# Up projection and embedding gate in seven half-sized products, weight sums made in DRAM, up and down in groups

## The chip, the cores and the metric

The kernel runs on one core of a Trainium2 chip. The metric is the device time of one execution in microseconds, as the median of several runs. The engines are named as the profile names them: PE is TensorE (matmuls), PEld its weight loads, DVE VectorE, ACT ScalarE, POOL GpSimd, SP SyncE. "Software transfers" are the DMA transfers that POOL issues; SP issues the others.

## The reference

One layer of a decoder on x of 512 tokens by 1024 channels, all in float32. A mixer with three attention branches comes first, then an output projection, a LayerNorm (LN1), and the part that is changed here:

```python
for i in range(DEPTH):            # DEPTH = 1
    m = mixer(x, w_in[i], ...)                                   # ends with merged @ w_out
    x = layer_norm(DEEPNORM_ALPHA * x + m, ln1_g[i], ln1_b[i])
    hid = jax.nn.relu(x @ w_up[i])                               # 1024 -> 4096
    c = jnp.square(hid) @ w_down[i]                              # 4096 -> 1024
    ple = jax.nn.sigmoid(x @ w_ple_gate[i]) * (p[i] @ w_ple[i])  # gate 1024 -> 1024, p has 256 channels
    x = layer_norm(DEEPNORM_ALPHA * x + c + ple, ln2_g[i], ln2_b[i])
```

## The kernel before, in words

**Precision.** Every fp32 operand is split in two parts: a high part (a cast, ACT, L227 for weights) and a low part (the operand less its high part, DVE, L229). A product is three matmuls: high by high, high by low, low by high (`mm3`, L86 to L89). A matmul has 128 x 128 weights and up to 512 columns.

**Items.** The program is a list of items, one per product tile. An item has a function that emits its matmuls into one PSUM bank (`mm`) and one that empties the bank (`ev`), which the main loop emits one item later. PSUM has two banks with the tag `mm` and six with the tag `at`. Between items the loop advances the attention's generators (`step`) and, after the output projection, those of LN1 (`pending`).

**Weights.** `load` puts a 512 KB piece of weights in a list, `fill` (L169) issues the loads in that order on SP's queue into `RAW` = 4 buffers named `raw`, and `split_next` (L215) makes the high and low part (`wh`, `wl`, `RING` = 7 of each). `pump` calls both, at most seven pieces ahead of the items that are done with theirs.

**Order.** The mixer's items end at `wout_at`. Then come the per-layer embedding p @ w_ple (`ple_items`, 8 items of 6 matmuls), the output projection (`wout_items`, 8 of 24), the embedding's gate (`pleg_items`, 8 of 24), the MLP, and a plain block at its end (`plain`). After each 128 tokens of the output projection `ln1_gen` runs LN1, whose reciprocal root is a pow on POOL (L462), then transposes x1 and splits it into `x1hT` and `x1lT`.

**MLP.** The up projection has 32 items (`up`), each 128 hidden channels by 512 tokens in 24 matmuls of 512 columns; ACT does Relu and Square into `hid`. The down projection takes the hidden channels in seven blocks of 512 and a plain one. A block uses the seven-product scheme for a 2 x 2 block matrix (Strassen's, in Winograd's form): with A the hidden tile and B the weights, each cut in 2 x 2, seven products p = 1 to 7 of half size replace eight. Products of sums need sums of weights: `total` with `add` (L195 to L205) makes four of them per block on DVE, as `wsum` 128x1024 tiles. The sums of hidden tiles are made on DVE by `left_first` and `left_rest`. Up items stand between the down items one by one.

**Transfers on POOL.** One pT tile (`pTraw`, issued at `wout_at` - 9), and at `wout_at` - 1 the constants `ln_g`, `ln_b` and eight tiles `xn` of the residual. The pows of the differential attention (L1148) are on POOL as well.

Of the kernel before, what the change touches and what calls it, by code (L numbers as in the profile page):

```python
# [55 lines left out]
def trunk(tc, a, out):  # L56
    nc = tc.nc
    es = ExitStack()
    with es:
# [7 lines left out]
        NSLOT = 42  # L67
# [74 lines left out]
        RING, RAW, NSUM = 7, 4, 3  # L142
        ORDERED, AHEAD = 17, 4
        loads, sums, chunks, placed = [], [], [], []
        st = {"dma": 0, "sum": 0, "split": 0}
# [6 lines left out]
        def total(s1, s2):  # L152

            s = {"of": (s1, s2), "w": s1["w"], "uses": 0}
            s1["uses"] += 1
            s2["uses"] += 1
            sums.append(s)
            return s
# [10 lines left out]
        def fill():  # L169
            while st["dma"] < len(loads):  # L170
                s = loads[st["dma"]]
                if not s["own"]:
# [19 lines left out]
                add()  # L192
            add()

        def add():  # L195
            while st["sum"] < len(sums) and (st["sum"] < NSUM or sums[st["sum"] - NSUM]["uses"] == 0):
                s = sums[st["sum"]]
                if any("raw" not in x for x in s["of"]):
                    break
                r = ring.tile([P, 1024], F32, name=nm("wsum"), tag="wsum", bufs=NSUM)  # L200
                s["raw"] = r[:, :s["w"]]
                nc.vector.tensor_add(s["raw"], s["of"][0]["raw"], s["of"][1]["raw"])
                for x in s["of"]:
                    x["uses"] -= 1
                st["sum"] += 1  # L205
# [9 lines left out]
        def split_next():  # L215
# [9 lines left out]
            for h, lo, a0, a1 in parts:  # L225
                raw = c["from"]["raw"][:, a0:a1]
                i = nc.vector.tensor_copy(h, raw) if c.get("dve") else nc.scalar.copy(h, raw)  # L227
                st["cast"] = getattr(i, "ins", i)
                i = nc.vector.tensor_sub(lo, raw, h.bitcast(F32))  # L229
                st["low"] = getattr(i, "ins", i)  # L230
# [290 lines left out]

        def ln1_gen(tt):
# [4 lines left out]
            q = slice(tt * P, tt * P + P)  # L527
            if not x1T:
                bh = one.tile([P, 8, 512], F32R, name="x1hT", tag="XH", bufs=1)
                bl = one.tile([P, 8, 512], F32R, name="x1lT", tag="XL", bufs=1)  # L530
                for k in range(8):
                    x1T[k], x1Tl[k] = bh[:, k, :], bl[:, k, :]
                x1T["b"], x1Tl["b"] = bh, bl
            for h in range(2):
                tp = at_bank()
                for b in range(4):
                    nc.tensor.transpose(tp[:, b * P:b * P + P], x1[tt, h][:, b * P:b * P + P], ident)
                o = x1T["b"][:, 4 * h:4 * h + 4, q]
                t3 = tp.rearrange("p (k t) -> p k t", k=4)
                nc.scalar.copy(o, t3)  # L540
                nc.vector.tensor_sub(x1Tl["b"][:, 4 * h:4 * h + 4, q], t3, o.bitcast(F32))
            ln1_done[tt] = True
# [24 lines left out]
        def pleg_items():  # L567
            for half in range(2):
                cs = [chunk(a["wg"][half, c].rearrange("p k n -> p (k n)"), 1024) for c in range(4)]
                for tt in range(4):  # L570
                    def mm(ps, tt=tt, cs=cs):
                        for k in range(8):
                            c = cs[k // 2]
                            s = slice((k % 2) * 512, (k % 2) * 512 + 512)
                            q = slice(tt * P, tt * P + P)
                            nc.tensor.matmul(ps, x1T[k][:, q], c["h"][:, s], start=k == 0, stop=False)  # L576
                            nc.tensor.matmul(ps, x1T[k][:, q], c["l"][:, s], start=False, stop=False)  # L577
                            nc.tensor.matmul(ps, x1Tl[k][:, q], c["h"][:, s], start=False, stop=k == 7)

                    def ev(ps, tt=tt, half=half):  # L580
                        g = slot("sg2")
                        nc.scalar.activation(g, ps, AF.Sigmoid)
                        nc.vector.tensor_mul(g, g, ple.pop((tt, half)))
                        t = x1[tt, half]
                        nc.vector.scalar_tensor_tensor(t, t, ALPHA, g, op0=OP.mult, op1=OP.add)
                        acc[tt, half] = t
                        if half and tt > 1:
                            nc.vector.tensor_sub(acc[tt - 2, 1], acc[tt - 2, 1], t)
                    item(cs if tt == 3 else [], mm, ev, need=cs)

        hraw = {}
# [8 lines left out]
        def mlp_items():  # L605
            nb = 7

            def up(f, free=True):
                c = chunk(a["wu"][f].rearrange("p k m -> p (k m)"), 1024)

                def mm(ps):
                    for k in range(8):
                        s = slice(k * P, k * P + P)
                        mm3(ps, c["h"][:, s], c["l"][:, s], x1T[k], x1Tl[k], k == 0, k == 7)

                def ev(ps):
                    t = slot("hid")
                    nc.scalar.activation(t, ps, AF.Relu)
                    nc.scalar.activation(t, t, AF.Square)
                    left_rest()  # L620
                    if f >= 4 * nb:
                        left[f] = split(t)
                        return
                    hraw[f] = t
                    if f % 2:
                        left_first(f // 2)
                item([c] if free else [], mm, ev)
                return c

            def split(t, cols=slice(0, 512)):  # L630
                h = slot("hh", F32R)
                lo = slot("hl", F32R)
                nc.scalar.copy(h[:, cols], t[:, cols])
                nc.vector.tensor_sub(lo[:, cols], t[:, cols], h[:, cols].bitcast(F32))
                return h, lo

            def left_first(pr):
                e, o = hraw[2 * pr], hraw[2 * pr + 1]
                s12 = slot("s12")
                nc.vector.tensor_sub(s12[:, HB], e[:, HC], o[:, HC])  # L640
                nc.vector.tensor_sub(s12[:, HC], e[:, HB], s12[:, HB])
                w = slot("hh", F32R)
                nc.scalar.copy(w[:, HB], e[:, HB])
                nc.vector.tensor_sub(w[:, HC], e[:, HB], w[:, HB].bitcast(F32))
                left[pr, 1] = (w[:, HB], w[:, HC])
                h, lo = split(s12)
                left[pr, 5] = (h[:, HB], lo[:, HB])
                left[pr, 6] = (h[:, HC], lo[:, HC])
                later.append((pr, s12))

            def left_rest():
                if not later:
                    return
                pr, s12 = later.popleft()
                e, o = hraw.pop(2 * pr), hraw.pop(2 * pr + 1)
                s34 = slot("s34")
                nc.vector.tensor_sub(s34[:, HB], e[:, HC], e[:, HB])
                nc.vector.tensor_sub(s34[:, HC], o[:, HB], s12[:, HC])
                for t, (p1, p2) in ((s34, (7, 3)), (o, (2, 4))):
                    h, lo = split(t)  # L660
                    left[pr, p1] = (h[:, HB], lo[:, HB])
                    left[pr, p2] = (h[:, HC], lo[:, HC])

            def down(b, p, r, c, free=()):
# [9 lines left out]
                def mm(ps):  # L674
                    q = slice(r * P, r * P + P)
                    for i in range(2):
                        h, lo = left[2 * b + i, p]
# [7 lines left out]
                def ev(ps):  # L685
# [3 lines left out]
                    if (p, r) in ((6, 0), (7, 0)):  # L689
                        left_rest()  # L690
# [17 lines left out]
            def plain(cs, c2, c3, c4):  # L708
# [6 lines left out]
                def part(tt, half, cc):  # L715
# [5 lines left out]
                    def mm(ps):  # L721
                        q = slice(r * P, r * P + P)
                        for i in range(2 if p else 0):
                            h, lo = left[2 * nb - 2 + i, p]
# [4 lines left out]
                        q = slice(tt * P, tt * P + P)  # L729
                        for i in range(4):  # L730
                            h, lo = left[4 * nb + i]
# [58 lines left out]
            for f in range(4):  # L790
                up(f)
            for b in range(nb):
                wd = a["wd"][b]
                ld = lambda i: load(wd[i].rearrange("p k n -> p (k n)"), 1024)
                up(4 * b + 4)
                s11 = ld(0)
                s12 = ld(1)
                t1 = total(s11, s12)
                c5 = chunk_of(t1)
                c1 = chunk_of(s11)  # L800
                down(b, 5, 0, c5)
                down(b, 1, 0, c1)
# [677 lines left out]
```

## Time and profile before

| | us |
|---|---|
| median of three runs (1083.58, 1085.79, 1085.93) | 1085.79 |
| span of the profiled execution, first to last instruction | 1082.1 |
| PE busy | 1070.5 |
| PEld busy | 892.7 |
| DVE busy | 691.8 |
| ACT busy | 477.5 |
| POOL busy | 31.3 |
| granted TensorE clock, mean | 0.998 |

How to read the profile's lines. A group line gives line, engine, operation, tile written <- tiles read, shape and count, then "busy us, mean ns of one", then the engine's idle time just before those instructions and what ended it. A waits line gives engine, tile and line, what it waited for, then total us, number of waits and the longest. A timeline line gives start, duration, engine, line and operation, and in brackets the idle time before and its cause. A DMA line gives tile <- source, the queue's engine, count, KB each and the median us from issue to landing. Durations of matmuls are those of one in the pipeline; how fast they follow one another is read from their starts.

### The profile page before, as it was taken

To read this page: it belongs to the slowest core of one execution; us is meant where nothing else is said; L and a number is where in the kernel's file an instruction comes from. 1 tells how busy PE (TensorE), PEld (TensorE's weight loads), DVE (VectorE), ACT (ScalarE), POOL (GpSimd) and SP (SyncE) were. 2 spreads that over 40 slices of the span, in tenths; PEclk is the share of its full clock that TensorE was granted. 3 is DMA by queue.
4 is the path that set the end of the run, shared out by engine and by line. 5 is a ranking of instruction groups with operands and counts; after the bars stand their busy time and mean duration, and the time that the engine had idled before them with its cause. 6 is when DMAs were issued, how large, how long until landed. Compare 5 with 4: busy or idle time off the path is not lost.

```text
span 1082.1 us, 13108 instructions
## 1 busy us (share of the span) xinstructions
PE 1070.5 (99%) x4991; PEld 892.7 (83%) x4991; DVE 691.8 (64%) x1246; ACT 477.5 (44%) x794; POOL 31.3 (3%) x55
## 2 busy tenths in 40 slices
PE   8999999999999999999999999999999999999997
PEld 6888788999888888888888888888888888888886
DVE  6887667547254757655444364866686686686676
ACT  6675545425232545464333332333555454454441
POOL 0000200000000000000000020110000000000000
PEclk9999999999999999999999999999999999999999
DMA  7432313132322113113232362253232332422402
GB/s 250 131 117 86 100 58 98 39 98 79 117 78 78 59 47 101 64 65 92 96 104 91 105 214 87 92 172 98 78 98 92 122 98 85 130 97 82 132 1 78
DMA packets 32431, 105.71 MB, mean 98 GB/s; under 512 B 4378, under 2 KB 5290, under 8 KB 32368
## 3 DMA queue, kind: packets, MB, share of 16 engines
q1 hardware_dynamic: 29424, 96.91, 27.3%
q0 software_dynamic: 2368, 7.05, 2.1%
q8 instruction: 39, 0.64, 0.2%
q10 hardware_dynamic: 576, 0.92, 0.2%
q14 instruction: 24, 0.20, 0.1%
HBM read 102.74 MB, written 2.12 MB: 97 GB/s over the span
## 4 chain that ended last, share of the span: by engine, by line
PE 96%; DVE 2%; ACT 1%; DMA 0%; issue 0%; DVEq 0%; SPq 0%
PE mm L87 17%; PE mm L88 17%; PE mm L89 17%; PE mm L339 3%; PE mm L341 3%; PE mm L340 3%; PE mm L681 2%; PE mm L683 2%; PE mm L682 2%; PE at L681 2%; PE at L683 2%; PE at L682 2%; PE mm L512 1%; PE mm L576 1%; PE mm L577 1%; PE mm L511 1%
## 5 line engine op out<-in xcount | busy, mean ns | idle before, releaser
L227 ACT CAST wh<-raw 128x1024 fp32r<-128x1024 f32 (+1 forms) x173 | 178.3, 1032 | 292.8 <-PE mm L88 223.5
L229 DVE TENSOR_TENSOR wl<-raw,wh 128x1024 fp32r<-128x1024 f32 (+1 forms) x173 | 206.0, 1197 | 104.5 <-ACT wh L227 100.8
L87 PE MATMUL mm<-xhT,wh 128*128 128x512 f32 x496 | 196.5, 396 | 0.0
L89 PE MATMUL mm<-xhT,wl 128*128 128x512 f32 x496 | 194.0, 391 | 0.0
L88 PE MATMUL mm<-xlT,wh 128*128 128x512 f32 x496 | 193.9, 391 | 0.0
L87 PEld LDWEIGHTS mm<-xhT,wh 128*128 128x128 f32 x496 | 93.2, 188 | 19.8 <-issue 1.4
L89 PEld LDWEIGHTS mm<-xhT,wl 128*128 128x128 f32 x496 | 93.1, 188 | 19.8 <-DVE wl L229 0.2
L88 PEld LDWEIGHTS mm<-xlT,wh 128*128 128x128 f32 x496 | 93.2, 188 | 17.8
L87 PE MATMUL mm<-x1hT,wh 128*128 128x512 f32 x256 | 99.6, 389 | 0.0
L88 PE MATMUL mm<-x1lT,wh 128*128 128x512 f32 x256 | 99.6, 389 | 0.0
L89 PE MATMUL mm<-x1hT,wl 128*128 128x512 f32 x256 | 99.6, 389 | 0.0
L339 PE MATMUL mm<-wh,xhT 128*128 128x512 f32 x160 | 64.7, 404 | 0.0
L341 PE MATMUL mm<-wh,xlT 128*128 128x512 f32 x160 | 63.1, 394 | 0.0
L340 PE MATMUL mm<-wl,xhT 128*128 128x512 f32 x160 | 62.9, 393 | 0.0
L89 PEld LDWEIGHTS mm<-x1hT,wl 128*128 128x128 f32 x256 | 48.1, 188 | 10.1
L88 PEld LDWEIGHTS mm<-x1lT,wh 128*128 128x128 f32 x256 | 48.0, 188 | 10.0
L87 PEld LDWEIGHTS mm<-x1hT,wh 128*128 128x128 f32 x256 | 48.0, 188 | 9.9
L227 ACT CAST wh<-wsum 128x1024 fp32r<-128x1024 f32 x28 | 29.5, 1054 | 52.4 <-PE mm L88 49.3
L229 DVE TENSOR_TENSOR wl<-wsum,wh 128x1024 fp32r<-128x1024 f32 x28 | 34.2, 1222 | 24.2 <-ACT wh L227 23.6
L341 PEld LDWEIGHTS mm<-wh,xlT 128*128 128x128 f32 x160 | 37.9, 237 | 3.9
L340 PEld LDWEIGHTS mm<-wl,xhT 128*128 128x128 f32 x160 | 38.1, 238 | 3.4
L339 PEld LDWEIGHTS mm<-wh,xhT 128*128 128x128 f32 x160 | 37.9, 237 | 3.5
(349 smaller groups left out, 1968.7 us busy)
## 6 DMA issues: line engine op xcount, KB each, us to landing
raw<-in_wt_dram SPq DMA_DIRECT2D x62, 512.0 KB, 3.4
raw<-in_wu_dram SPq DMA_DIRECT2D x32, 512.0 KB, 3.4
raw<-in_wd_dram SPq DMA_DIRECT2D x32, 512.0 KB, 3.3
raw<-in_wv_dram SPq DMA_DIRECT2D x20, 512.0 KB, 3.4
raw<-in_wb_dram SPq DMA_DIRECT2D x8, 512.0 KB, 3.3
raw<-in_wo_dram SPq DMA_DIRECT2D x8, 512.0 KB, 3.9
raw<-in_wg_dram SPq DMA_DIRECT2D x8, 512.0 KB, 4.0
rawx<-in_xT_dram SPq DMA_DIRECT2D x8, 256.0 KB, 5.6
```

The costliest lines, as they stand in the source:

```text
L87: nc.tensor.matmul(ps, wh, xh, start=start, stop=False, skip_group_check=True)
L88: nc.tensor.matmul(ps, wh, xl, start=False, stop=False, skip_group_check=True)
L89: nc.tensor.matmul(ps, wl, xh, start=False, stop=stop, skip_group_check=True)
L227: i = nc.vector.tensor_copy(h, raw) if c.get("dve") else nc.scalar.copy(h, raw)
L229: i = nc.vector.tensor_sub(lo, raw, h.bitcast(F32))
L339: nc.tensor.matmul(ps, x1, c["h"][:, s], start=k == 0, stop=False)
L340: nc.tensor.matmul(ps, x1, c["l"][:, s], start=False, stop=False)
L341: nc.tensor.matmul(ps, x2, c["h"][:, s], start=False, stop=k == 7)
L511: nc.tensor.matmul(ps, h[:, q], c["l"][:, s], start=False, stop=False)
L681: nc.tensor.matmul(ps, h[:, q], c["h"][:, s], start=go, stop=False, skip_group_check=True)
L682: nc.tensor.matmul(ps, h[:, q], c["l"][:, s], start=False, stop=False, skip_group_check=True)
L683: nc.tensor.matmul(ps, lo[:, q], c["h"][:, s], start=False, stop=end, skip_group_check=True)
```

## The change

- **Up** becomes eight blocks of seven products. A block has 512 hidden channels; its weights are cut in 2 x 2 (input channels, hidden channels), x1 likewise (channels, tokens). A product has 24 matmuls of 256 columns (two halves j of one bank). The products come in the order 1, 2, 6, 5, 7, 3, 4, and several accumulate into one bank one after the other ("chained"): 1, 6, 7, 4 in bank A, 2 in B, then 5, 3 in a new B. After 1, 6 and 5 the bank's state is copied out by ACT (`cut`), and the parts after 2, 7 and 3 are the sum or difference of a copy and a bank (DVE).
- **Gate**: the same with 512 columns, 14 items of 12 matmuls, chained in `at` banks X and Y; product 2 has an `mm` bank.
- **x1**: `ln1_gen` makes the seven operands (`xs`, and places in `x1hT` and `x1lT`) from the transposed tiles, two 128-token rows at a time; the first two rows keep raw copies (`xr`).
- **Weight sums**: four for each of 15 blocks and eight for the gate, 68 in all. A sum is a DRAM tile: POOL issues a copy of the first operand (16x8192), then an accumulating transfer of the second (512 rows of 1 KB). From item 14 on the loop issues one per item and one in the half step of odd items. Each waits for the third weight cast before its place. The loads then read a sum like other weights. DVE's `wsum` adds and their buffers are gone; the tag "s" has 48 slots for 42.
- **Groups**: all seven up products of a block b + 1, then the 14 down products of block b (in pairs 2 and 1, 5 and 6, 3 and 7, then 4 alone). The hidden tiles' sums and splits are a queue of small jobs (`later`), one or two taken per item.
- **Order**: the output projection first, gate products 1 and 2, the per-layer embedding, gate products 5, 6, 7, 3, 4, the MLP. pT is loaded from `wout_at` + 2 into slots; LN2's constants are loaded 12 items before the plain block.

POOL at the LN loads, before: the last pow of the attention's norm (`ms`), then pT and the constants.

```order
L1148 TENSOR_TENSOR ms_4314<-ms_4314,mhalf 128x4
L981 DMA pTraw<-in_pT_dram 128x1024
L450 DMA ln_g_5479<-in_ln_g_dram 128x512
L450 DMA ln_g_5480<-in_ln_g_dram 128x512
L450 DMA ln_b_5483<-in_ln_b_dram 128x512
```

After, the last rows ahead of the same loads:

```order
L165 DMA total_133<-total_132 16x8192
L165 DMA total_134<-in_wu_dram 16x8192
L165 DMA total_133<-in_wu_dram 512x256
L165 DMA total_134<-in_wu_dram 512x256
L165 DMA total_135<-total_133 16x8192
L448 DMA ln_g_5667<-in_ln_g_dram 128x512
L448 DMA ln_g_5668<-in_ln_g_dram 128x512
```

Between the last `ms` pow and `ln_g` now stand 42 transfers of sums (total_114's copy to total_135's copy); pT has moved behind the eight `xn`.

POOL at LN1, before: the last `xn` load, then the four pows of the LN (`lr`).

```order
L495 DMA xn_5501<-in_xn_dram 128x512
L462 TENSOR_TENSOR lr_5778<-lr_5778,mhalf 128x1
L462 TENSOR_TENSOR lr_5832<-lr_5832,mhalf 128x1
L462 TENSOR_TENSOR lr_5884<-lr_5884,mhalf 128x1
L462 TENSOR_TENSOR lr_5960<-lr_5960,mhalf 128x1
L450 DMA ln_g_6271<-in_ln_g_dram 128x512
```

After:

```order
L165 DMA total_138<-in_wd_dram 16x8192
L165 DMA total_137<-total_136 16x8192
L165 DMA total_137<-in_wd_dram 512x256
L460 TENSOR_TENSOR lr_5900<-lr_5900,mhalf 128x1
L460 TENSOR_TENSOR lr_5939<-lr_5939,mhalf 128x1
L460 TENSOR_TENSOR lr_6010<-lr_6010,mhalf 128x1
L165 DMA total_138<-in_wd_dram 512x256
L165 DMA total_139<-total_137 16x8192
L165 DMA total_139<-in_wd_dram 512x256
L460 TENSOR_TENSOR lr_6091<-lr_6091,mhalf 128x1
L448 DMA ln_g_9360<-in_ln_g_dram 128x512
```

The first three pows follow six transfers of sums and the pT loads, and the last three transfers of sums stand between the third pow and the fourth.

PE where a down product is followed by an up item, before (the down product's bank mm_6506 has six matmuls, the up item's mm_6520 has 24):

```order
L681 MATMUL mm_6506<-wh_6257,hh_6440 128x512
L682 MATMUL mm_6506<-wl_6258,hh_6440 128x512
L683 MATMUL mm_6506<-wh_6257,hl_6441 128x512
L87 MATMUL mm_6520<-x1hT,wh_6304 128x512
L88 MATMUL mm_6520<-x1lT,wh_6304 128x512
L89 MATMUL mm_6520<-x1hT,wl_6305 128x512
```

After, at the end of one of the down groups (mm_8427 is the second row half of product 4, and mm_8415 with six matmuls, the first, stands right before it):

```order
L831 MATMUL mm_8427<-wh_8274,hh_8213 128x512
L832 MATMUL mm_8427<-wl_8275,hh_8213 128x512
L833 MATMUL mm_8427<-wh_8274,hl_8214 128x512
L744 MATMUL mm_8442<-x1hT,wh_8308 128x256
L745 MATMUL mm_8442<-x1lT,wh_8308 128x256
L746 MATMUL mm_8442<-x1hT,wl_8309 128x256
```

The up item's matmuls have 256 columns, and both products ahead of it use `mm` banks, where before an `at` product stood between two of them.

The diff, cut to its core:

```diff
+        def total(s1, s2):
+            t = dram.tile([P, 1024], F32, name=nm("total"), tag=nm("total"), bufs=1)
+            sums.append((t, s1, False))
+            sums.append((t, s2, True))
+            return t
+        casts = deque(maxlen=3)
+        def add():
+            if not sums:
+                return
+            t, s, more = sums.popleft()
+            i = nc.gpsimd.dma_start(t, s, accum_op=OP.add, max_dma_last_dim=1024) if more else nc.gpsimd.dma_start(t, s)
+            tc.add_manual_dep(getattr(i, "ins", i), casts[0].name, mybir.DependencyInfo(
+                mybir.DependencyClass.Sync, mybir.DependencyReason.DATA), reason="one sum at a time")
...
-                nc.vector.tensor_add(s["raw"], s["of"][0]["raw"], s["of"][1]["raw"])
...
+            for p, k0, t in ((1, 0, B0), (2, 4, B0), (4, 4, B1), (5, 0, B1)):
+                ops[p] = [[(b[:, k0:k0 + 4, t], 0, 4)] for b in (bh, bl)]
...
+            if tt < 2:
+                split_x1(1, r, tps[0])
+                split_x1(2, r, tps[1])
+                raws[r] = [raw(0), raw(1)]
...
+            def up_item(b, p):
+                c = chunk(up_w[b][p], 1024)
+                def bank():
+                    if p in (1, 2, 5):
+                        held["A" if p == 1 else "B"] = mm_bank()
+                    return held["B" if p in (2, 5, 3) else "A"]
+                def mm(ps):
+                    for j in range(2):
+                        o = ps[:, 256 * j:256 * j + 256]
+                        for k in range(4):
+                            s = slice((4 * j + k) * P, (4 * j + k) * P + P)
+                            h, lo = operand(p, k, slice(0, 256))
+                            first = j == 0 and k == 0 and p in (1, 2, 5)
+                            last = j == 1 and k == 3 and p in (2, 3, 4)
+                            nc.tensor.matmul(o, c["h"][:, s], h, start=first, stop=False, skip_group_check=True)
+                            nc.tensor.matmul(o, c["h"][:, s], lo, start=False, stop=False, skip_group_check=True)
+                            nc.tensor.matmul(o, c["l"][:, s], h, start=False, stop=last, skip_group_check=True)
+                def ev(ps):
+                    if p in (1, 5, 6):
+                        t = slot("cut")
+                        nc.scalar.copy(t, ps)
+                        cut[p] = t
+                        return
...
+            ups(0)
             for b in range(nb):
...
+                ups(b + 1)
+                first = len(items)
+                c234 = downs(b)
...
-        ple_items()
-        wout_items()
-        pleg_items()
+        wout_items()
+        wg_items((1, 2), wg_w)
+        ple_items()
+        wg_items((5, 6, 7, 3, 4), wg_w)
         mlp_items()
...
-            if n == wout_at - 9:
+            if n >= 14:
+                add()
+            if n == wout_at + 2:
                 load_pT()
...
             for _ in it["mm"](ps) or ():
+                step()
+                if n >= 14 and n % 2:
+                    add()
```

More of the change, by code (lines that the diff above doesn't have):

```diff
@@ L171, in fill @@
                 s = loads[st["dma"]]
+                while any(t is s["src"] for t, _, _ in sums):
+                    add()
                 if not s["own"]:
@@ L191, in fill @@
                 st["dma"] += 1
[L192 to L205, printed above, removed]
         tie = []
@@ L526, in ln1_gen @@
             yield
[L527 to L533, printed above, removed]
+            yield
+            if not ops:
+                x1_places()
+            r = tt % 2
+            tps = []
             for h in range(2):
@@ L565, in ple_items @@
                     item([cs[half]] if tt == 3 else [], mm, ev, need=cs)
[L567 to L589, printed above, removed]
@@ L606, in mlp_items @@
             nb = 7
[L608 to L628, printed above, removed]
@@ L631, in split, with down_weights @@
+            def down_weights(b):
+                down_w[b] = weights([a["wd"][b, i].rearrange("p k n -> p (k n)") for i in range(4)])
+            def split(t):
                 h = slot("hh", F32R)
                 lo = slot("hl", F32R)
-                nc.scalar.copy(h[:, cols], t[:, cols])
-                nc.vector.tensor_sub(lo[:, cols], t[:, cols], h[:, cols].bitcast(F32))
+                nc.scalar.copy(h, t)
+                nc.vector.tensor_sub(lo, t, h.bitcast(F32))
                 return h, lo
[L637 to L649, printed above, removed]
@@ L666, in down, with jobs @@
+            def jobs(n):
+                for _ in range(n):
+                    if later:
+                        later.popleft()()
+            def down(b, p, r, c, free=(), njobs=0):
                 last = b == nb - 1
@@ L1301, in trunk @@
         BANKS = 8
-        HALF = True
         last = [-99]
```

326 lines of the change are left out of this document (234 added, 92 removed).

## The prediction

> **What bounds the kernel now.** I read the page first (busy time, chain), then TensorE's waits, then a window of the MLP stage, then the stretch in which matmuls have 256 columns.
>
> ```profile
> span 1082.1 us, 13108 instructions
> PE 1070.5 (99%) x4991; PEld 892.7 (83%) x4991; DVE 691.8 (64%) x1246; ACT 477.5 (44%) x794; POOL 31.3 (3%) x55
> ...
> PE 96%; DVE 2%; ACT 1%; DMA 0%; issue 0%; DVEq 0%; SPq 0%
> ...
> L87 PE MATMUL mm<-x1hT,wh 128*128 128x512 f32 x256 | 99.6, 389 | 0.0
> ```
> ```profile
> PE at L320 <- ACT wh L227: 1.8, 1, 1.8
> PE at L847 <- DVE rel L883: 1.3, 1, 1.3
> ```
> ```profile
> 800.00:900.00 100.00, 100.00 (x443) 82.81 (x442) 71.21 (x97) 49.30 (x67) 0.00 (x0) 1.00 0.33 110
> ```
>
> TensorE (PE) is busy 99% of the span, it makes up 96% of the chain, and its two longest waits are 1.8 and 1.3 us. So a matmul taken away is worth its full time, and nothing else is worth anything until it makes TensorE wait. In the window 800 to 900 (columns: busy us and instructions of PE, PEld, DVE, ACT, POOL, then granted clock 1.00, DMA share 0.33, GB/s) TensorE never pauses: 100 us / 443 = 225.7 ns from one 512-column matmul to the next; the 389 ns in the group's row is the length of one in the pipeline. DVE has 29% spare there and ACT 51%. The median of the runs, 1085.8, stands 3.7 us over the profiled span; I carry those 3.7 over.
>
> **The matmuls.** The up projection loses 32 x 24 = 768 matmuls of 512 columns (the row x256 above is one of its three terms) and gains 8 blocks x 7 products x 24 = 1344 of 256 columns. What one of these costs, the end of the down projection shows:
>
> ```profile
> 1071.29 0.28 PE L734 MATMUL at<-wh,hh 128*128 128x256 f32 x1
> ...
> 1074.05 0.28 PE L736 MATMUL at<-wh,hl 128*128 128x256 f32 x1
> ```
> ```profile
> 1071.41 0.19 PEld L736 LDWEIGHTS at<-wh,hl 128*128 128x128 f32 x1
> 1071.53 0.19 PEld L734 LDWEIGHTS at<-wh,hh 128*128 128x128 f32 x1
> ```
>
> From 1071.29 to 1074.05 stand 24 starts: 2.76 / 23 = 120 ns each. The weight loads take 0.19 us but start 0.12 apart, so they overlap one another and the matmuls. Up: 768 x 0.2257 = 173.3 us becomes 1344 x 0.120 = 161.3 us, 12.0 less. Seven eighths of the matmul columns would be 151.7 us; 7 ns on each short matmul eat 9.6 us of the 21.6 that the count promises. That 21.6, with half a long matmul (113 ns) each, is the lower bound of the price. The upper bound is a weight load that no longer overlaps, 192 ns, 96.7 us more than the sum; the row is the same form of instruction, so I take 120. The gate keeps 512 columns and goes from 192 to 168 matmuls: 24 x 0.2257 = 5.4 us less. Down and everything earlier keep their matmuls. Sum on TensorE: -17.4 us.
>
> The Trainium skill, "TensorE: Matmul & The Clock Gate", section "The mechanism", says that a weight load overlaps matmuls in flight only when their row groups differ. Here all are the full 128 rows, so by it each short matmul would wait for its own load. The rows above disagree: loads of 0.19 us at a pitch of 0.12.
>
> **Casts, low parts, evacuations.**
>
> ```profile
> L227 ACT CAST wh<-raw 128x1024 fp32r<-128x1024 f32 x165 | 173.3, 1052 | 273.7 <-PE mm L88 204.4 <-PE mm L683 20.4 <-PE mm L512 19.2
> L227 ACT CAST wh<-wsum 128x1024 fp32r<-128x1024 f32 x28 | 29.5, 1054 | 52.4 <-PE mm L88 49.3 <-PE at L683 2.7 <-PE mm L578 0.3
> L619 ACT ACTIVATE hid<-hid 128x512 f32<-128x512 f32 x32 | 20.3, 635 | 1.0
> L618 ACT ACTIVATE hid<-mm 128x512 f32<-128x512 f32 x32 | 18.9, 589 | 0.0
> L633 ACT CAST hh<-s 128x512 fp32r<-128x512 f32 x28 | 17.3, 619 | 12.4 <-DVE s L641 9.1 <-DVE s L658 3.3
> ```
> ```profile
> L229 DVE TENSOR_TENSOR wl<-raw,wh 128x1024 fp32r<-128x1024 f32 x165 | 200.5, 1221 | 95.0 <-ACT wh L227 91.3 <-PE at L1138 2.8
> L229 DVE TENSOR_TENSOR wl<-wsum,wh 128x1024 fp32r<-128x1024 f32 x28 | 34.2, 1222 | 24.2 <-ACT wh L227 23.6
> L688 DVE TENSOR_TENSOR xn<-xn,mm 128x512 f32<-128x512 f32 x50 | 34.0, 681 | 7.0 <-PE mm L683 7.0
> L634 DVE TENSOR_TENSOR hl<-s,hh 128x512 fp32r<-128x512 f32 x28 | 19.2, 687 | 4.3 <-ACT hh L633 4.2
> L202 DVE TENSOR_TENSOR wsum<-wsum,raw 128x1024 f32<-128x1024 f32 x14 | 17.1, 1225 | 26.6 <-DMA raw<-in_wd_dram 26.6
> L202 DVE TENSOR_TENSOR wsum<-raw,raw 128x1024 f32<-128x1024 f32 x14 | 17.1, 1218 | 1.0 <-DMA raw<-in_wd_dram 1.0
> ```
>
> After the change one block of up and down is 7 x 24 x 0.120 + 84 x 0.2257 = 39.1 us of TensorE. In it ACT has 14 casts (14.7 us), three copies out of PSUM at about 0.59 (1.8), four Relu and Square (4.9) and seven splits of hidden tiles (4.3): 25.7 us, 66%. DVE has 14 low parts (17.1), three evacuations of up and eight of down (7.5), four differences and seven low parts of hidden tiles (7.6): 32.2 us, 82%. The four sums per block (4.9 us) are gone from DVE. Both fit, so I cost them at nothing on average. The cover is thin inside the up group: a product lasts 24 x 0.120 = 2.88 us, and its successor but one writes the same bank; a copy that comes behind a cast and a Relu with its Square is through after 1.05 + 1.22 + 0.59 = 2.86 us. Bounds: 0, or 0.3 us on each of 56 products, 17 us. I take 0 inside a group, since of seven casts per 20.2 us few meet the pair. Where a down group ends and an up group begins, two products of 1.36 us (6 x 0.226) stand back to back ahead of a bank that DVE must free behind two low parts (2.4 us): 0 to 1.35, taken as 0.3, six times: 2 us.
>
> **The sums by transfer.** 68 sums are 136 transfers of 512 KB on POOL's queue, a copy and an accumulate each. No row of before shows an accumulate. The nearest transfers:
>
> ```profile
> raw<-in_wu_dram SPq DMA_DIRECT2D x32, 512.0 KB, 3.4
> ...
> sh<-rv POOLq DMA_DIRECT2D x8, 256.0 KB, 4.6
> raw<-in_wb_dram SPq DMA_DIRECT2D x8, 256.0 KB, 2.6
> xn<-in_xn_dram POOLq DMA_DIRECT2D x8, 256.0 KB, 8.5
> ...
> pTraw<-in_pT_dram POOLq DMA_DIRECT2D x1, 512.0 KB, 3.9
> ```
> ```profile
> 497.02 1.01 POOL L1148 TENSOR_TENSOR ms<-ms,mhalf 128x4 f32<-128x4 f32 x1 [24.22 <-DVE ms L1147]
> 626.92 0.59 POOL L981 DMA_DIRECT2D pTraw<-in_pT_dram  x1 [128.89 <-PE mm L89]
> 635.99 1.07 POOL L450 DMA_DIRECT2D ln_g<-in_ln_g_dram  x2 [8.48 <-PE mm L89]
> ...
> 646.52 0.54 POOL L495 DMA_DIRECT2D xn<-in_xn_dram  x1 [0.91 <-DMA ln_b<-in_ln_b_dram]
> 683.44 1.00 POOL L462 TENSOR_TENSOR lr<-lr,mhalf 128x1 f32<-128x1 f32 x1 [36.38 <-DVE lr L461]
> ```
> ```profile
> 654.31 0.69 DVE L98 COPY ple<-mm 128x512 f32<-128x512 f32 x1 [2.03 <-PE mm L559]
> ...
> 659.75 0.69 DVE L516 SCALAR_TENSOR_TENSOR xn<-xn,mm 128x512 f32<-128x512 f32 x1 [3.13 <-PE mm L512]
> ```
>
> POOL is idle where the transfers go, but its queue is in order: behind 42 of them (21 sums) since the last pow at 497.0 stand the loads of ln_g, ln_b and xn that began at 636.0, so they have 139 us. A later transfer of a chain waits at the head of the queue for the landing of the one it reads. In eight transfers (four sums of a block) POOL stands through about three copies and two accumulates: the budget is 139 x 8 / 42 = 26.5 us. With 3.9 us for a copy (pTraw) and some 0.75 for an issue, an accumulate may land in 7.0 us; each microsecond more delays the LN loads by 5.25 blocks x 2 = 10.5 us. Bounds for the accumulate: 3.9, if it is a copy, and twice the slowest row of that queue, 17. I take 6, between twice the SP load (two reads) and sh, whose rows are as short: then nothing is late. DMA load: 71 MB more over some 600 us, about 120 GB/s beside the 100; with four raw buffers the SP loads stand 4 x 5.4 us (24 x 0.2257) ahead of use, against 3.4.
>
> By "DMA: Bandwidth & Descriptors", section "Anatomy of one DMA", in the Trainium skill, a software DMA takes 2.0 us and its bytes at 436 GB/s: 3.2 us here as an estimate, 4.4 for double bytes; by it nothing would be late and the sum stays as below. No trace of this case shows an accumulate yet.
>
> **What is moved around the first LN.** The per-layer embedding (8 items, 10.9 us by 48 x 0.2257) goes behind the output projection, which now starts right after the branches. The last split of the merged tile had that cover; without it 0 to 5.4 us (one item), taken as 1.5. xn is needed 10.9 us earlier than 659.75, so at 648.9, and one item later before a bank stops TensorE: 654.3. It lands at 638.1 + 8.5 = 646.6, so about 8 us of slack. The pow of the fourth LN now stands behind three transfers that wait for casts and a copy's landing: about 6 us late, of which items of the gate on other rows hide half: 0 to 6, taken as 2.5. Transposes and combined operands of x1 (longer on ACT and DVE than before): 0 to 4, taken as 1. Stalls: 2 + 1.5 + 2.5 + 1 = 7 us.
>
> Sum: 1085.8 - 17.4 + 7 = 1075.4; I say 1075 (span 1071).
>
> **Rivals.**
> A, the forecast: 0 to 12 us of stalls, 1068 to 1080.
> B, sums or POOL a little late, or thin covers met now and then: 12 to 17 us of stalls, 1080 to 1086.
> C, slower, by the POOL queue: an accumulate that lands in more than 7.0 us makes the LN loads late, the output projection stops at its second item and everything after shifts. The 8 us of slack and the 10.4 us of net gain are used up at 7.0 + 18.4 / 10.5 = 8.75 us; at 10 us it is 31.5 - 8 = 23.5 of stall, 1099; at 12, 1120. For it: xn's 8.5 us on the same queue, and sh's 4.6 for half the bytes, 9 for all. Against: the 8.5 is time in a row of queued loads, and pTraw alone took 3.9.
> D, slower or same: up products stop for their banks 0.2 to 0.4 us each, or the pitch of short matmuls is 133 ns in long runs: 11 to 22 us, 1086 to 1097. For it the 2.86 against 2.88; against it that ACT is idle a third of the block.
> E, the weight load binds: 1344 x 0.192 = 258 us, about 1172.
>
> **Numbers.** A 0.60; B 0.12; C 0.20; D 0.07; E 0.01. About 0.2%, 2.2 us, is what a measurement of this kernel can tell from no change. Faster is A and half of B, 0.66; same is half of B and 0.02 of D, 0.08; slower 0.26. The range 1066 to 1100 holds A, B, D and the near part of C; its lower end is the full gain with no stall (1068.4), less 2 us for a slightly shorter pitch. A's own range is 1068 to 1080.
>
> **What would show it.** TensorE busy about 1053 us with 5313 instructions listed, short matmuls 120 ns apart; no `wsum` rows on DVE; POOL's issues of sums about 3 us apart and the LN loads still at about 636; the first LN's pows 8 to 12 us earlier than 683, except the fourth; waits of TensorE on DVE for `mm` at the starts of up groups, 0.3 us each. I am wrong if the chain holds DMA or POOL in the stretch 500 to 700 (C), or if TensorE waits for ACT on `mm` in many short pieces between 720 and 1040 (D).

## The result and the profile after

The changed kernel takes 1126.25 us (median of 4 runs, 1124.38 to 1129.46) against 1084.84 before (4 runs): ratio 1.0391, 95% interval 1.0368 to 1.0413. The forecast was 1075 in 1066 to 1100. The kernel is slower by the mechanism of rival C, at a size that C's own working did not give.

The page of the changed kernel, its busy line, clock, chain and software queue:

```profile
span 1122.7 us, 14695 instructions
PE 1064.6 (95%) x5543; PEld 911.4 (81%) x5543; DVE 719.7 (64%) x1264; ACT 528.8 (47%) x866; POOL 136.9 (12%) x192
...
PEclk9999999999999999999999995999999999999998
...
q0 software_dynamic: 40464, 78.36, 32.4%
...
PE 49%; DMA 5%; DVE 3%; issue 2%; ACT 1%; POOL 1%; DVEq 0%; POOLq 0%; ACTq 0%
```

TensorE's busy time fell from 1070.5 to 1064.6 us, where about 1053 was forecast, yet the span grew by 40.6. The loss is idle time of TensorE and, behind it, matmuls that run at half clock (without the sums, in the first experiment below, TensorE is busy for 1055.4 us). Its waits in the changed kernel (total, times, longest):

```profile
PE mm L508 <- DVE xn L514: 29.8, 3, 28.1
PE at L1277 <- DVE lg L1272: 3.9, 2, 3.7
PE at L651 <- DVE x1lT L541: 3.0, 1, 3.0
PE mm L744 <- DVE xn L838: 2.3, 6, 0.4
PE at L1309 <- DVE on L1303: 2.1, 1, 2.1
PE at L1044 <- issue: 2.0, 1, 2.0
...
PE mm L744 <- DVE cut L756: 1.2, 1, 1.2
```

One wait of 28.1 us stands out: a matmul of the output projection (L508) waits for a bank that DVE empties with `xn` (L514). DVE is only the messenger; what it waits for is seen in POOL's timeline of the changed kernel:

```profile
656.97 0.91 POOL L165 DMA_DIRECT2D total<-in_wu_dram  x1
667.30 1.01 POOL L165 DMA_DIRECT2D total<-in_wu_dram  x1 [9.42 <-DMA total<-in_wu_dram]
673.26 0.52 POOL L165 DMA_DIRECT2D total<-total  x1 [4.95 <-DMA total<-in_wu_dram]
...
677.71 1.03 POOL L165 DMA_DIRECT2D total<-in_wu_dram  x1 [3.43 <-DMA total<-total]
...
684.62 1.14 POOL L448 DMA_DIRECT2D ln_g<-in_ln_g_dram  x2
685.75 1.08 POOL L448 DMA_DIRECT2D ln_b<-in_ln_b_dram  x2
686.83 1.62 POOL L493 DMA_DIRECT2D xn<-in_xn_dram  x3
```

The LN loads that began at 635.99 before begin at 684.62. Ahead of them POOL stands idle 9.42, 4.95 and 3.43 us at a time, each time for the landing of the transfer that the next one reads. The prediction's own sign of being wrong is there: the chain of the changed kernel runs through these landings (start, us, what).

```profile
656.97 9.71 DMA total<-in_wu_dram
...
667.30 5.46 DMA total<-in_wu_dram
...
673.26 4.16 DMA total<-total
```

The first and the third are copies, the second is an accumulate. The changed kernel's windows around it and one of the MLP (PE busy is the first figure behind the stretch and its length, granted clock the third from the end):

```profile
640.00:660.00 20.00, 20.00 (x90) 16.57 (x89) 13.45 (x17) 5.65 (x7) 4.65 (x6) 1.00 0.90 231
660.00:680.00 20.00, 5.99 (x27) 4.63 (x25) 0.00 (x0) 0.00 (x0) 3.89 (x5) 0.74 0.66 164
680.00:700.00 20.00, 5.91 (x14) 4.65 (x15) 1.38 (x2) 0.00 (x0) 10.00 (x18) 0.50 1.08 274
...
900.00:1000.00 100.00, 99.25 (x651) 90.95 (x651) 75.47 (x91) 64.68 (x87) 0.00 (x0) 1.00 0.60 185
```

By stages, from first matmul to first matmul (in the kernel before the embedding's items come first in the middle stage, in the changed one the output projection): the mixer ends about 12.0 us later (643.0 to 654.9), the stage from output projection to the gate's end takes 137.7 us instead of 101.9, and the MLP with the tail 330.0 instead of 337.2. Sum: 12.0 + 35.8 - 7.2 = 40.6.

### The profile page after: what moved, and what is told of

Its sections match the earlier page's. It is cut to its first block, busy times and chain, and to the rows that moved or that the text cites. A ratio compares the mean times of both kernels' runs of the same rounds, so it can differ in the third digit from the quotient of the medians.

```text
span 1122.7 us, 14695 instructions
## 1 busy us (share of the span) xinstructions
PE 1064.6 (95%) x5543; PEld 911.4 (81%) x5543; DVE 719.7 (64%) x1264; ACT 528.8 (47%) x866; POOL 136.9 (12%) x192
## 3 DMA queue, kind: packets, MB, share of 16 engines
q1 hardware_dynamic: 36768, 123.66, 33.5%
## 4 chain that ended last, share of the span: by engine, by line
PE 49%; DMA 5%; DVE 3%; issue 2%; ACT 1%; POOL 1%; DVEq 0%; POOLq 0%; ACTq 0%
PE mm L88 6%; PE mm L87 6%; PE mm L89 6%; PE mm L744 5%; PE mm L746 5%; PE mm L745 5%; PE at L833 2%; PE at L831 2%; PE at L832 2%; PE mm L831 2%; PE mm L832 2%; PE mm L833 2%; DMA total<-total 1%; DMA total<-in_wu_dram 1%; DVE wl L227 1%
## 5 line engine op out<-in xcount | busy, mean ns | idle before, releaser
L224 ACT CAST wh<-raw 128x1024 fp32r<-128x1024 f32 (+1 forms) x231 | 238.9, 1036 | 313.0 <-PE mm L88 167.1
L227 DVE TENSOR_TENSOR wl<-raw,wh 128x1024 fp32r<-128x1024 f32 (+1 forms) x231 | 276.9, 1203 | 138.4 <-ACT wh L224 132.5
L744 PE MATMUL mm<-x1hT,wh 128*128 128x256 f32 x256 | 73.0, 285 | 3.5 <-DVE xn L838 2.3
L745 PE MATMUL mm<-x1lT,wh 128*128 128x256 f32 x256 | 72.4, 283 | 0.0
L746 PE MATMUL mm<-x1hT,wl 128*128 128x256 f32 x256 | 72.4, 283 | 0.0
L165 POOL DMA_DIRECT2D total<-in_wu_dram x48 | 42.2, 904 | 154.7 <-DMA total<-total 59.7
L165 POOL DMA_DIRECT2D total<-in_wd_dram x42 | 38.4, 969 | 140.2 <-DMA total<-total 41.8
L508 PE MATMUL mm<-wh,mh 128*128 128x512 f32 x64 | 26.5, 414 | 29.8 <-DVE xn L514 29.8
L744 PE MATMUL mm<-xs,wh 128*128 128x256 f32 x192 | 54.3, 283 | 0.0
L745 PE MATMUL mm<-xs,wh 128*128 128x256 f32 x192 | 54.3, 283 | 0.0
L746 PE MATMUL mm<-xs,wl 128*128 128x256 f32 x192 | 54.3, 283 | 0.0
L744 PEld LDWEIGHTS mm<-x1hT,wh 128*128 128x128 f32 x256 | 49.1, 192 | 6.0 <-issue 6.0
```

The lines of the kernel that those rows point to most:

```text
L165: i = nc.gpsimd.dma_start(t, s, accum_op=OP.add, max_dma_last_dim=1024) if more else nc.gpsimd.dma_start(t, s)
L744: nc.tensor.matmul(o, c["h"][:, s], h, start=first, stop=False, skip_group_check=True)
L745: nc.tensor.matmul(o, c["h"][:, s], lo, start=False, stop=False, skip_group_check=True)
L746: nc.tensor.matmul(o, c["l"][:, s], h, start=False, stop=last, skip_group_check=True)
```

## The experiments

Theory 1: the sums are late on POOL's in-order queue, and what stands behind them (LN loads, pows) makes TensorE wait. Theory 2: the sums' bytes fill the DMA engines (share 0.9) and make every transfer late, whatever the order. Theory 3: the new order of items stalls by itself. The kernel before took 1083.4 to 1083.9 us beside the runs below.

**No sums at all.**

```diff
-            t = dram.tile([P, 1024], F32, name=nm("total"), tag=nm("total"), bufs=1)
-            sums.append((t, s1, False))
-            sums.append((t, s2, True))
-            return t
+            return s1
```

> Leaves out all 136 transfers of the weight sums: the loads read the first operand in place of the sum. Theory 1 (the sums are late on POOL's in-order queue and hold up what stands behind them: the LN loads and the pows) and theory 2 (the sums fill the DMA engines, share 0.9 in 500 to 660, and every load is late): both 1072 to 1078, with TensorE waiting under 8 us in all between 640 and 800. Theory 3 (the new order of output projection, gate and embedding stalls TensorE by itself, whatever the sums do): 1090 to 1110.

1072.3 us, ratio 0.9896 (0.9881 to 0.9911). Its table of waits has nothing long for TensorE:

```profile
PE mm L741 <- DVE xn L835: 2.3, 6, 0.4
PE at L315 <- ACT wh L221: 1.6, 1, 1.6
```

Theory 3 is out: new products, chains and order gain 11 us, and the sums cost 54. (This kernel reads one operand in place of each sum, so it shows a time and not the layer's output.)

**The LN loads past the sums.** The loads of ln_g, ln_b, xn and pT issued by SP (one of three such edits):

```diff
...
-                nc.gpsimd.dma_start(t, a["xn"][:, tt, 512 * h:512 * h + 512])
+                nc.sync.dma_start(t, a["xn"][:, tt, 512 * h:512 * h + 512])
...
```

> The loads of ln_g, ln_b, xn and pT are issued by SP instead of POOL; the pows stay behind the sums. Theory 1: xn lands before the output projection's first evacuation, so the 28.1 us wait and the slow matmuls after it go (about 31 us), but LN1's pows now wait for the queue to drain to about 710, which costs 10 to 18 us after the output projection; the 11 us lost in the mixer stay: 1100 to 1112. Theory 2: the loads come late from SP as well, 1115 or more.

1119.2 us, ratio 1.0325 (1.0297 to 1.0354): only 7 us less than the changed kernel, above the 1112 that theory 1 gave. The wait moved instead of going. TensorE's three longest waits of this run, then two lines of its POOL timeline:

```profile
PE at L556 <- DVE xn L464: 19.6, 1, 19.6
PE at L1277 <- DVE lg L1272: 5.7, 2, 5.6
PE at L1309 <- DVE on L1303: 3.5, 1, 3.5
```
```profile
718.63 1.05 POOL L165 DMA_DIRECT2D total<-in_wd_dram  x1 [3.61 <-DMA total<-total]
719.31 0.97 POOL L460 TENSOR_TENSOR lr<-lr,mhalf 128x1 f32<-128x1 f32 x1
```

The output projection runs through, then the transposes of LN1 (L556) wait 19.6 us for a pow that comes to its turn at 719.31, behind the sums. I had put that at 710. The first 18 us are lost in the mixer already, where I had 11: set against the kernel without sums, the same matmuls start 18.3 us later from 465 us on. By itself this run fits theory 2 nearly as well; the next one decides.

**The pows past the sums, too.** The LN loads stay on SP; bytes, rows and chain of the sums stay as they are. The edit is made at both places that have a pow; one is shown.

```diff
...
-            nc.gpsimd.tensor_tensor(r, r, mhalf, OP.pow)
+            nc.scalar.activation(r, r, AF.Ln)
+            nc.scalar.activation(r, r, AF.Exp, scale=-0.5)
...
```

> As the last one, and the pows of LN1 and of the attention's norm are made on ACT (Ln, then Exp with -0.5, two table loads each), so that POOL's queue holds nothing but sums and what belongs to the tables. The sums' traffic is unchanged. Theory 1: the mixer's 11 us and the wait for the pows go, table loads cost up to 5: 1076 to 1088. Theory 2: 1105 or more, since the same bytes move in the same time.

1083.4 us, ratio 0.9999 (0.9981 to 1.0017), single runs from 1078.6 to 1089.7. The accumulates land no sooner (7.2 us, median, against 7.1), and still 43 us are gone. Windows of this run, whose traced execution took 1079.4 us and so is one of its faster ones:

```profile
450.00:500.00 50.00, 50.00 (x252) 42.19 (x251) 27.78 (x67) 30.16 (x65) 9.17 (x12) 1.00 0.78 189
...
600.00:640.00 40.00, 40.00 (x178) 33.15 (x177) 18.71 (x24) 12.10 (x16) 6.60 (x9) 1.00 0.83 224
640.00:660.00 20.00, 20.00 (x89) 16.54 (x89) 8.55 (x12) 2.73 (x3) 3.11 (x4) 1.00 1.02 336
```

TensorE does not pause beside a DMA share of 0.83 to 1.02, and the attention's stage 450 to 500, where the changed kernel lost 3.7 us, is whole. This settles between the theories: the order on POOL costs 43 us of the 54. The other 11 are parted only in the traced execution, which has 5.8 us more than the kernel without sums: 5.0 of them arise between 693 and 703, where DVE waits for the new pows of LN1 on ACT (2.69 and 2.29 us) and TensorE for DVE (2.6). ACT has 17 table loads of 1.28 us in this run, and four in the changed kernel. What the slower executions lose besides is not shown.

**Larger rows.**

```diff
-            i = nc.gpsimd.dma_start(t, s, accum_op=OP.add, max_dma_last_dim=1024) if more else nc.gpsimd.dma_start(t, s)
+            i = nc.gpsimd.dma_start(t, s, accum_op=OP.add, max_dma_last_dim=8192) if more else nc.gpsimd.dma_start(t, s)
```

> The accumulates move rows of 8 KB (64 rows) instead of 1 KB (512 rows); nothing else. If the price of an accumulate is that of its rows, it lands in 5 us or less instead of 7.2, POOL stands 2 x 2.2 us less per eight transfers, about 75 us less over all, so the LN loads are on time: 1075 to 1088. If its price is that of its bytes (two reads, one write), it lands in 7 us as before: 1120 to 1130.

1117.6 us, ratio 1.0311 (1.0284 to 1.0338), 9 us less than the changed kernel and 2 us under the second range. The accumulates land in 7.0 us (median; 7.1 with rows of 1 KB), as that range supposed: the price is not that of the rows.

**Copies alone**, without the accumulates (a single run):

```diff
-            sums.append((t, s2, True))
```

> Leaves out the 68 accumulates; the copies stay in their chain. Theory 1: three copies waited for per block, 13.5 us and 68 transfers in all, never late: 1072 to 1078. If the copies' bytes alone crowd the loads: over 1085.

1076.6 us. The copies by themselves, 36 MB, hold nobody up: the last output lands at 1069.2 us, 1.1 earlier than without any sums, and what the run has over that kernel comes behind it.

**Two chains at a time.** The transfers of two blocks are dealt out alternately; their places in the queue and their number stay.

```diff
+        def two_chains(m):
+            x, y = list(sums)[m:m + 8], list(sums)[m + 8:m + 16]
...
+            for i in (0, 1, 4, 2, 5, 3, 6, 7):
+                sums.extend([x[i], y[i]])
...
```

> The same 136 transfers in the same places of POOL's queue, but the sums of two blocks (an up and a down block) are dealt out alternately, so that a transfer seldom waits at the head of the queue for the one just before it. If POOL's time is the sum of landings waited for in one chain (theory 1), sixteen transfers cost about what eight did, the sums keep pace with the items, the LN loads begin at 640 to 650, and the kernel takes 1073 to 1085. If the DMA engines limit the sums (theory 2: share 0.9), two transfers in flight take twice as long each and nothing is won: 1115 to 1127.

1092.7 us, ratio 1.0082 (1.0063 to 1.0102): 33.5 us less than the changed kernel, though not inside 1073 to 1085. The LN loads begin at 648; from 504.1 on the 42 transfers ahead of them took 3.5 us each. What POOL waits for first in this run, then its DMA issues:

```profile
POOL total L173 <- ACT wh L232: 342.7, 45, 90.3
```
```profile
raw<-in_wt_dram SPq DMA_DIRECT2D x62, 512.0 KB, 6.1
total<-in_wu_dram POOLq DMA_DIRECT2D x48, 512.0 KB, 9.4
total<-in_wd_dram POOLq DMA_DIRECT2D x42, 512.0 KB, 8.0
```

POOL now mostly waits for the casts that pace it, and for landings of the sums 140 us in all, where the changed kernel has 316. So the chain of landings was what held it. A part of theory 2 holds: with two chains in flight an accumulate takes 9.1 us (median of the 68; the rows above count copies with them), and the mixer's weight loads (in_wt) 6.1, against 5.4 in the changed kernel and 3.4 before. Set against the kernel without sums matmul by matmul, the traced execution loses 4 us by 118 us (the one-hot tables `oh`, which POOL loads, stand behind the first sums), 10 between 655 and 678 (`xn` is still late) and 5 from 711 to 716 (LN1's last row).

With rows of 8 KB as well:

> As two_chains, with accumulates in rows of 8 KB. Theory 1: equal to two_chains or up to 5 us faster, since the POOL spends 0.25 us less on each accumulate's issue and the last pow is a little earlier: 1072 to 1082. Theory 2: 1105 to 1120, as the rows alone gave 9 us.

1089.2 us, ratio 1.0042 (1.0025 to 1.0059), and with the LN loads on SP besides:

> As two_chains_8k, with ln_g, ln_b, xn and pT loaded by SP; the pows stay on POOL behind few transfers, and no table loads are added. Theory 1: 1072 to 1078, the time without sums plus the wait for the fourth pow. Theory 2: as the runs before, over 1100.

1081.9 us, ratio 0.9985 (0.9973 to 0.9998). Both are above what theory 1 gave; in the second, the start of the tables behind the first sums still cost TensorE 1.1 us and clock (0.93 in 100 to 150), and around 700, at LN1's last row, it falls 4.5 us further behind the kernel without sums.

**Fewer sums per item.** I then tried the rate instead of the chain.

```diff
-                if n >= 14 and n % 2:
-                    add()
```

> The program puts one transfer per item on POOL's queue instead of three in two items (5.4 us of TensorE per transfer instead of 3.6 in the mixer); chain, rows and loads as in the changed kernel, the first still at item 14; the rest of the sums stand between and behind the LN1 pows. Theory 1: the queue needed 4.2 us per transfer, so with 5.4 it keeps pace: the LN loads begin at 636 to 645 and the 28 us wait is gone; the pows of LN1 wait for one transfer each: 1074 to 1084. Theory 2 (bytes in flight): fewer bytes per us, better too, 1080 to 1100. If neither, and the order on POOL is not it: over 1110.

1118.0 us, ratio 1.0331 (1.0296 to 1.0365). The expectation failed: LN loads at 670. By its own words a time over 1110 speaks against the order on POOL, but that supposed a queue that keeps pace, and this one did not.

On top of that edit, a later start, a pause around LN1, and then one transfer in every second item:

```diff
-            if n >= 14:
+            if 26 <= n < wout_at - 2 or n >= wout_at + 15 and n % 2:
                 add()
```

> One transfer per item from item 26 on (behind the mixer's tables), none from two items before the output projection to the 15th item after it (LN1's loads and pows stand alone), then one in every second item of the MLP, where POOL had nothing to do. Theory 1: nothing waits behind a sum any more, LN loads at 636, first LN1 pow at about 672 as without sums: 1072 to 1077, faster than the kernel before. Theory 2: the accumulates in the MLP stage compete with 185 GB/s of weight loads there and TensorE waits for casts: 1080 to 1095.

1104.3 us, ratio 1.0193 (1.0162 to 1.0224): above both ranges. The LN loads begin at 663, and TensorE's waits have new ones in the MLP (L744, L885). The traced execution is the slowest of six, 1113.6 us. TensorE's longest waits, then one of SP's:

```profile
PE mm L508 <- DVE xn L514: 12.2, 2, 11.7
PE mm L744 <- ACT cut L751: 11.0, 2, 9.6
PE at L1309 <- DVE on L1303: 5.5, 2, 4.6
PE mm L885 <- DVE wl L227: 2.8, 1, 2.8
```
```profile
SPq L196 <- DMA total<-in_wd_dram: 36.3, 3, 18.9
```

In the MLP the load of a sum now stands ready before the sum is made, up to 18.9 us: a late chain holds up its own readers too, which neither theory had.

The error was in my 5.4 us per item: that is an item's matmuls. Where the queue fell behind, ACT makes 31 casts in 143 us (before, 500 to 643), one per item, 4.6 us each, while earlier it is 21 in 150, 7.1 us. Here one chain took 4.6 us per transfer (37 from 500.6 to 670.2 in one_per_item) and 4.8 in spread (33 from 505.7 to 663.1): no slack. With rows of 8 KB the same schedule is just under the mark, and the LN loads begin at 635:

> As spread, with accumulates in rows of 8 KB. Theory 1: the same within 2 us, 1071 to 1077, since no one waits for POOL. Theory 2: a few us faster than spread.

1079.6 us, ratio 0.9957 (0.9944 to 0.9970), 25 us less than spread, where I had 2 or a few. Larger rows were worth 9, 3.5 and 25 us in three settings; that this depends on how near the queue is to its limit fits, and is not shown apart.

**The pieces together.**

```diff
+            if 26 <= n < wout_at - 2 or n >= wout_at + 15 and n % 3 == 0:
+                add()
...
+                if 26 <= n < wout_at - 2 and n % 2:
+                    add()
```

> The pieces that helped, together: two chains dealt out alternately, rows of 8 KB, sums only from item 26 on, none from two items before the output projection to the 15th item after it, then one in every third item of the MLP; in the mixer three in two items as in the changed kernel. Theory 1 (what waits behind the sums on POOL costs the time): LN loads at 636 to 642, LN1 pows as without sums, TensorE's waits as without sums: 1073 to 1078. Theory 2 (bytes beside the weight loads cost by themselves): 1078 to 1084, since the bytes are the same as in spread_8k.

1073.9 us, ratio 0.9905 (0.9889 to 0.9922): faster than both kernels, inside theory 1's range, and within 1.6 us of the kernel without sums. All 136 transfers are made, so their bytes by themselves cost little in this order. Two lines of its POOL timeline:

```profile
632.09 1.41 POOL L456 DMA_DIRECT2D ln_g<-in_ln_g_dram  x2
...
675.88 1.01 POOL L468 TENSOR_TENSOR lr<-lr,mhalf 128x1 f32<-128x1 f32 x1 [28.86 <-DVE lr L467]
```

The first LN1 pow finds POOL idle for 28.86 us before it, where the changed kernel had it come at 724.7.

## Why the prediction was wrong

**The matmuls: right.** A short matmul follows the last after 120 ns in the changed kernel too (792.80, 792.92, 793.04 and so on). The weight load's rival E is out, and with it, for this form, the sentence of the Trainium skill ("TensorE: Matmul & The Clock Gate", section "The mechanism") that a load overlaps matmuls only when the row groups differ; the same section also lets a load into the background weight buffer go ahead of matmuls, which these times do not contradict. Only the count was added up wrongly: 4991 - 768 + 1344 - 24 is 5543, as the profile lists, and not 5313.

**The stalls outside the sums: right in sum.** The kernel without sums has a span 10.6 us under the one before; the prediction had -17.4 + 7 = -10.4. That they agree is luck: of the 7 us, 2.5 were for a pow behind transfers, which this kernel does not have. The stage around LN1 lost 1.3 us (97.7 us with the gate's 5.4 less, against 101.9), where 2.5 were left for it; the mixer lost 0.8, and the MLP gained 7.2 instead of 10. The six waits at up groups are there at 0.38 each (2.3 in all), and one of 1.2 besides.

**The step that failed: the price of the sums on POOL.** "An accumulate may land in 7.0 us ... I take 6 ... then nothing is late." The budget, 26.5 us for eight transfers, stood. One period of the queue, from 639.02 to 673.26, waits for three copies and two accumulates, as counted: copy 4.7, accumulate 7.6, copy 5.0, copy 10.3, accumulate 6.0. That is 20.0 us for three copies, where I took 11.7 from one transfer that had POOL's queue to itself, and 13.6 for two accumulates, where I took 12.0. So the greater error was the plain copy: the first of the next block is issued right behind an accumulate and lands 1.2 us after it, 9.7 us from its issue (whether the queue or the DMA engines make it wait is not parted here). Over all 42 transfers the queue needed 4.18 us each (684.07 - 512.89 over 41) and had 3.3. In these 171 us POOL stood idle about 83 us until a copy landed, where the prediction's count gives 5.25 x 11.7 = 61, and 52 until an accumulate did, where it gives 63. By C's own sum, which prices the accumulate alone, 7.1 us would have made the LN loads 1 us late; they came 48.6 late.

The changed kernel's DMA rows (us to landing last):

```profile
total<-in_wu_dram POOLq DMA_DIRECT2D x48, 512.0 KB, 7.2
total<-in_wd_dram POOLq DMA_DIRECT2D x42, 512.0 KB, 7.0
total<-total POOLq DMA_DIRECT2D x34, 512.0 KB, 4.5
```

The first two rows mix accumulates with the copies that read a weight. Taken one by one from the trace, the 68 accumulates have a median of 7.1 us and the 68 copies one of 6.7: 4.5 for those that read another sum, 7.3 for those that read a weight. The estimate by the Trainium skill's page "DMA: Bandwidth & Descriptors", section "Anatomy of one DMA" (3.2 us a copy, 4.4 for double bytes), is below all of these; the shortest copy took 3.7.

**C was sized too small for a second reason.** C priced the wait at the LN loads. The pows of the attention's norm stood behind sums as well: they came at 420.8, 450.5, 485.1 and 509.0 instead of 410.4, 440.1, 471.8 and 497.0, and the mixer ended 12.0 us late. DVE waits for the first two, and what TensorE waits for is made behind them (`lg` at L1272 came at 453.7):

```profile
422.23 0.69 DVE L1303 TENSOR_TENSOR on<-at,ms 128x512 f32<-128x512 f32 x1 [3.67 <-POOL ms L1301]
...
451.95 0.69 DVE L1303 TENSOR_TENSOR on<-at,ms 128x512 f32<-128x512 f32 x1 [3.64 <-POOL ms L1301]
```

Set against the kernel without sums, the same matmuls start 2.0 us later at 110 us (the tables `oh` behind the first sums), 3.9 more at 423 to 427 and 4.9 more at 454 to 457, these two with a half clock behind the wait; from there to 655 nothing is added, so the last two pows cost nothing by themselves. The prediction counted the fourth LN pow and none of these. And the wait at the LN loads cost more than its length, as the changed kernel's timeline of TensorE shows:

```profile
694.09 0.79 PE L508 MATMUL mm<-wh,mh 128*128 128x512 f32 x1 [28.11 <-DVE xn L514]
694.69 0.63 PE L509 MATMUL mm<-wl,mh 128*128 128x512 f32 x1
695.11 0.63 PE L510 MATMUL mm<-wh,ml 128*128 128x512 f32 x1
...
700.67 0.40 PE L509 MATMUL mm<-wl,mh 128*128 128x512 f32 x1
```

After 28 us without work matmuls follow each other at 0.43 us instead of 0.227 until 700.2, which costs about 3 us more.

**The range.** C had a chance of 0.20, and its far part was left outside. The range ends where C has 10 us for an accumulate (1099), though C itself gave 1120 at 12 us and the bound that the prediction had set was 17; and C kept the copy at 3.9 us throughout, though sh had taken 4.6 for half the bytes on the same queue.

## What to carry to other kernels

Work that is moved to an idle engine is not free if that engine's queue is in order and the work waits for its own landings: count the waits of the chain, price them by transfers that move beside others, and hold the sum against the time that the queue has in that stage, not against the mean. Then list what stands behind it, pows of 1 us included. Where the chain is the limit, two interleaved chains and a pause around the stage that needs the queue, here with larger rows, gave back nearly all (1126 to 1074 us).

## What the runs showed of the hardware

Medians of the 68 accumulates and 68 copies of a run, taken one by one from the traces: a 512 KB accumulate from DRAM into DRAM lands in 7.1 us beside the weight loads, in 6.5 to 7.0 with rows of 8 KB, in 9.1 with two chains in flight, and in 7.8 to 8.0 with both; a DRAM copy of the same size takes 3.7 at the least and 5.2 where there are only copies, 6.7 among the changed kernel's accumulates. A DMA share of 0.85 over 150 us (500 to 650) did not make TensorE pause in the kernel with only sums on POOL. An instruction or a load that stands behind such a transfer on POOL waits for the landing too: the first pow of LN1 came at 724.7 and not at 673.1 as without sums, the LN loads at 684.6 and not at 636.0 as before. What lands behind it is late as well: three loads of `oh` (66 KB) that POOL issued from 102.6 on, behind two sums, landed from 110.4 to 110.8, right after the second of these at 110.3; without sums each landed in 2.3 us at most.

The granted clock read 0.50 from 669.4 to 700.2, while the last matmul before the gap began at 665.6 and the next at 694.1, so the first 6.1 us of work ran at half clock. The Trainium skill, "TensorE: Matmul & The Clock Gate", part 1, gives half rate after an idle window and full rate after a busy one, with windows of about 3.4 us that run on whether work comes or not. That agrees: 669.4 to 700.2 is nine times 3.4, work began within the eighth window, and the ninth was the first full one.
